# The first sequence's paged values beside the last head's attention, its key pairs afterwards

## The chip, the core and the metric

The kernel runs on one core of a Trainium2 chip. The time is that of one execution on the device in microseconds, from runs of the whole program. One core has five engines that take their instructions in order and wait for each other by semaphores: PE (matrix products), DVE (vector operations), ACT (pointwise functions and copies), POOL (further vector operations) and SP, which here issues nearly all of the transfers between HBM and the on-chip memory.

## The reference

One layer is computed for two batches. The prompt has 1024 rows and 16 meta rows; eight samples have one row each and attend to 4096 past positions, which lie in pages of 128 positions at places that a page table names. Cut to what matters:

```
proj = rms_norm(x) @ w_in                        # q, k, v and the convolution's two inputs
a    = softmax(q1 k1) - lam * softmax(q2 k2)     # 4 heads, two maps each, ALiBi, causal
o    = a @ v                                     # prompt: own keys; sample: 32 pages of keys and values
mix  = concat(rms_norm(o), silu(layer_norm(conv(u)))) @ w_out
x    = x + rms_norm(mix)
y    = x + rms_norm((silu(h @ w_gate) * (h @ w_up)) @ w_down),  h = rms_norm(x)
```

All data are float32. The large products split each operand into a high and a low part and add three products.

## The kernel before

The program is recorded in Python in one long order, and a scheduler then sets the order on each engine by simulated times and priorities; on the chip each engine keeps that order. Three stages matter here.

The **attention** of the prompt runs over 4 heads and 8 blocks of 128 rows (n = 0 to 31; the last head is n = 24 to 31). For a block, PE makes the scores `S` (L507, L508), DVE adds the bias and finds the row's extreme (L509), ACT takes the exponential (L515), DVE joins the two maps (L526), PE transposes the result (`AT`, L534), ACT copies it (L538), and PE multiplies it with the values into `o` (L548). After four blocks, ACT copies `o` to `oh` and squares it (L557, L562), POOL takes the power (`or`, L564), ACT scales (L566), PE transposes (`oT`, L571) and ACT writes `mo` (L573). Beside the last head the eight parts of w_out are loaded (`wo0r` to `wo7r`, on SP, L132) and split by ACT (`wo0H` and on, L138) and POOL (`wo0L` and on, L140).

The **output projection** takes the 8 blocks with 48 products each (tile `mo`, L149 to L151, the same helper as in all large products). Its input rows are loaded as `mx` and split by ACT into `mH` (L900) and by DVE into `mL` (L901). The **FFN** then makes the gate, up and down products (`pg`, `pu`, `dn`), with weights that SP streams in.

The **paged attention** of the eight samples is spread over all of this by a generator, `dec_units`. One unit is a pair of pages, two transfers of 256 KB that SP issues (L665). A key pair is multiplied with the query on POOL (L680, two instructions) and summed on DVE (L690); each sum is recorded only after the next pair's product. A value pair waits until two pairs are there, and then PE makes their four products side by side (`pv`, L732, called a page group here). With one group done, as many key pairs follow as the group had value pairs. Each sequence has 16 key pairs and 16 value pairs. Between a sequence's keys and its values stand a maximum over all partitions on POOL (L707) and the exponential.

How many units are recorded at a place is set by rates: `rate_b` per block of attention (one entry per head), `rate_c` per block of the output projection, `rate_d` per step of the FFN, until all units are used up; then the samples' own rows follow at `rate_s`. At the end of the third head 23 key pairs are recorded, 16 of the first sequence and 7 of the second. A flag, `kv_n[1]`, is false until the last head has been recorded; while it is false, pages go to four buffers, afterwards also to the buffers of the attention's probabilities.

Of the kernel before, what the change touches and what calls it, by code (L numbers as in the profile page):

```python
# [46 lines left out]
def tile_layer(ctx: ExitStack, tc: tile.TileContext, I, O, cfg):  # L47
# [7 lines left out]
    at = ctx.enter_context(tc.tile_pool(name="at", bufs=cfg["at"]))  # L55
# [7 lines left out]
    kv_n = [0, False]  # L63
# [25 lines left out]
    def pdec(name):  # L89
        return ps.tile([P, 512], F32, tag="d", name=name, bufs=cfg["nd"])  # L90
# [564 lines left out]
    def page_pair(src, b, pg, name):  # L655
        t = kv(name)[:, :1024].rearrange("p (i n) -> p i n", i=2)
        for i in range(2):
            n = b * NPG + pg + i
            lds, (v,) = nc.values_load_multi_w_load_instructions(
                pts[0:1, n : n + 1], engines=[SP], min_val=0, max_val=n_pool - 1  # L660
            )
            if len(page_dmas) >= 8:
                for ld in lds:
                    tc.add_manual_dep(ld.ins if hasattr(ld, "ins") else ld, page_dmas[-8], behind, reason="few registers at once")
            x = D.dma_start(t[:, i, :], src[bass.DynSlice(v, 1)].rearrange("o p f -> (o p) f"))  # L665
            if cfg["anchor"] and i == 0:
                tc.add_manual_dep(x.ins if hasattr(x, "ins") else x, point["now"], behind, reason="paced by the prompt's work")
            page_dmas.append(x.ins.name if hasattr(x, "ins") else x.name)
        return t

    def dec_scores(b, st):
        qB = dec.tile([P, 512], F32, tag="qB", name=f"qB{b}")
        D.dma_start(qB, qsD[b].partition_broadcast(P))
        s = dec.tile([P, NPG + 1, 8], F32, tag="s", name=f"s{b}", bufs=3)
        st[b] = s
        for pg in range(0, NPG, 2):
            kt = page_pair(ck, b, pg, f"k{b}_{pg}")
            n = b * NPG // 2 + pg // 2
            for i in range(2):
                x = G.tensor_tensor(kt[:, i, :], kt[:, i, :], qB, op=ALU.mult)  # L680
            products.append((s[:, pg : pg + 2, :], kt))
            if len(products) > cfg["rlag"]:
                head_sums(x)
            yield b
# [3 lines left out]
    def head_sums(after):  # L688
        s, kt = products.pop(0)
        x = V.tensor_reduce(  # L690
            s.rearrange("p a c -> p (a c)"), kt.rearrange("p a (c d) -> p (a c) d", d=HD), axis=AX.X, op=ALU.add
        )
        if after is not None:
            tc.add_manual_dep(x.ins, after.ins.name, behind, reason="sums behind a later product")

    def dec_max(b, st):
        s = st[b]
        V.tensor_tensor(
            s[:, :NPG, :].rearrange("p g (h j) -> p (g h) j", j=2),
            s[:, :NPG, :].rearrange("p g (h j) -> p (g h) j", j=2),  # L700
            dbias.rearrange("p g h -> p (g h)").unsqueeze(2).to_broadcast([P, NPG * NH, 2]), op=ALU.add,
        )
        V.tensor_copy(s[:, NPG, :], selfs[:, b, :])
        m = smt(f"dm{b}", 8, 2)
        V.tensor_reduce(m, s.rearrange("p g c -> p c g"), axis=AX.X, op=ALU.max)
        mg = smt(f"dg{b}", 8, 2)
        G.partition_all_reduce(mg, m, P, bass.bass_isa.ReduceOp.max)  # L707
        st[b] = s, mg

    def dec_exp(b, st):  # L710
        s, mg = st[b]
        V.tensor_tensor(s, s, mg.unsqueeze(1).to_broadcast([P, NPG + 1, 8]), op=ALU.subtract)
        S.activation(s, s, AF.Exp)
        st[b] = s

    def dec_total(b, s):
        V.tensor_reduce(dsum[:, b, :], s.rearrange("p g c -> p c g"), axis=AX.X, op=ALU.add)
        V.tensor_tensor(selfa, selfa, s[:DB, NPG, :], op=ALU.add)

    def dec_values(b, st):  # L720
        a = st.pop(b)
        pv = pdec(f"pv{b}")
        vs = []
        for pg in range(0, NPG, 2):
            if not vs:
                size = min(cfg["vgrp"] if kv_n[1] else 2, (NPG - pg) // 2)
            vs.append((pg, page_pair(cv, b, pg, f"v{b}_{pg}")))
            if len(vs) == size:
                for q, vt in vs:
                    for i in range(2):  # L730
                        g = (q + i) % 4
                        x = T.matmul(  # L732
                            pv[32 * g : 32 * g + 8, :], lhsT=a[:, q + i, :], rhs=vt[:, i, :],
                            start=q + i < 4, stop=q + i >= NPG - 4, tile_position=(0, 32 * g),
                        )
                        if vt is not vs[-1][1]:
                            tc.add_manual_dep(x.ins, page_dmas[-1], together, reason="pages side by side")
                vs = []
            if pg == NPG // 2:
                dec_total(b, a)  # L740
            yield 0 if vs else size
        pvs = dec.tile([P, 512], F32, tag="gs", name=f"pvs{b}", bufs=2)
        for g in range(4):
            S.copy(pvs[32 * g : 32 * g + 8, :], pv[32 * g : 32 * g + 8, :])
            S.dma_start(pvD[b, g], pvs[32 * g : 32 * g + 8, :])

    def dec_units():
        st = {}
        ks = (b for bb in range(DB) for b in dec_scores(bb, st))
        nk, ready, exped, at = 0, 0, 0, []  # L750
        per = NPG // 2

        def softmaxes(all_=False):
            nonlocal ready, exped
            while "k" in nat and ready < (nk - len(products)) // per:
                dec_max(ready, st)
                at.append(nk)
                ready += 1
            while exped < ready and (all_ or nk >= at[exped] + cfg["elag"]):
                dec_exp(exped, st)  # L760
                exped += 1

        def keys(n):
            nonlocal nk
            for _ in range(n):
                if nk < DB * per:
                    next(ks)
                    nk += 1
                    if nk == DB * per:
                        while products:  # L770
                            head_sums(None)
                    softmaxes(nk == DB * per)
                    yield

        yield from keys(per + cfg["lag"])
        while "k" not in nat:
            yield "wait"
        softmaxes(True)
        for b in range(DB):
            for n in dec_values(b, st):  # L780
                yield
                yield from keys(n)

    dgen = dec_units()
    dst = {"done": False}

# [601 lines left out]
    lag=7, rlag=1, elag=2,  # L1388
    xn_g=(), wi_first=1, wi_e=(13, 17), sq=0,
    behind=-400, w0=7, w1=7, wi_n=1, anchor=1, wi_v=(8, 9, 10, 11, 12), taps=11, conv=400, r2_g=1, hb=5,  # L1390
    vgrp=2, fing=5, ml_g=0, fend=22, cst=0, db=3, cn=6, scn=12, wo0=27, wor=2, c0=7,
    at=8, slabs=35, kv=4, p=6, dve_mul=0, rate_b=(1, 1.25, 1, 0.75), rate_c=1, rate_d=2.45, rate_s=2.2,
    ffn_l=lambda nc: nc.vector,
)
_INS = [
# [39 lines left out]
```

## Time and profile before

| | us |
|---|---|
| median of 3 runs (range) | 1439.78 (1434.59 to 1439.84) |
| the profiled execution, whole | 1440.69 |
| its span, from the first to the last instruction | 1438.8 |
| PE busy | 1357.1 (94%) |
| DVE, POOL, ACT busy | 860.9, 595.2, 551.2 |

The span is what the trace covers; some 1.9 us lie around it. PE is busy nearly all the time, so a stretch in which PE waits is where something else sets the time, and a stretch in which it doesn't is as long as PE's work in it. [...]

### The profile page before, as it was taken

What the parts mean: (1) busy time and instruction counts of PE and PEld (TensorE: products, weight loads), DVE (VectorE), ACT (ScalarE), POOL (GpSimd) and SP (SyncE); (2) the same over time, 40 slices, a digit from 0 to 9 for tenths busy, and PEclk for the clock granted to TensorE, in tenths of its full rate; (3) what the DMA queues carried; (4) which work ended last, traced back from release to release, by engine and by line L of the source; (5) the groups of instructions that cost most, each with busy time, mean ns of one, the idle gap of its engine ahead of it and who ended that gap; (6) DMA issues with size and microseconds to landing.
All of it is one profiled execution on the core that took longest, in us unless ns stands there. A gap on an engine that the chain in (4) does not pass through costs nothing.

```text
span 1438.8 us, 21552 instructions
## 1 busy us (share of the span) xinstructions
PE 1357.1 (94%) x6960; PEld 1057.1 (73%) x6960; DVE 860.9 (60%) x1403; ACT 551.2 (38%) x1112; POOL 595.2 (41%) x479
## 2 busy tenths in 40 slices
PE   5999899989869999999999989999999989999997
PEld 5999799979747787777776757676776765666666
DVE  5689996936684567566645465654653374452158
ACT  6566878797764345113021121312121112211122
POOL 4598867445372113745545455464530000000023
PEclk9999999999889999999999999999999999999999
DMA  8211015226535548678867857777677656763454
GB/s 246 86 59 38 27 55 163 75 96 192 170 98 193 171 148 269 211 259 260 262 226 235 265 199 249 235 257 264 204 263 221 214 163 218 229 190 125 147 195 172
DMA packets 199677, 264.34 MB, mean 184 GB/s; under 512 B 16423, under 2 KB 99816, under 8 KB 199557
## 3 DMA queue, kind: packets, MB, share of 16 engines
q1 hardware_dynamic: 188912, 254.40, 54.3%
q10 hardware_dynamic: 10653, 8.57, 1.8%
q8 instruction: 55, 0.90, 0.3%
q14 instruction: 57, 0.47, 0.1%
HBM read 245.92 MB, written 17.48 MB: 183 GB/s over the span
## 4 chain that ended last, share of the span: by engine, by line
PE 59%; SPq 3%; DMA 3%; issue 3%; DVE 3%; POOL 2%; ACT 1%; POOLq 0%; DVEq 0%; ACTq 0%
PE dn L149 5%; PE pu L149 5%; PE dn L150 5%; PE dn L151 5%; PE pu L151 5%; PE pu L150 5%; PE pg L149 5%; PE pg L150 5%; PE pg L151 5%; PE pv L732 4%; PE mo L151 2%; PE mo L149 2%; PE mo L150 2%; DMA v<-in_cache_v 2%; SPq L665 2%
## 5 line engine op out<-in xcount | busy, mean ns | idle before, releaser
L680 POOL TENSOR_TENSOR k<-k,qB 128x512 f32<-128x512 f32 x256 | 353.5, 1409 | 230.2 <-DMA k<-in_cache_k 176.3
L690 DVE TENSOR_REDUCE s<-k 128x16 f32<-128x1024 f32 x128 | 154.8, 1213 | 101.1 <-POOL k L680 100.9
L956 ACT CAST wH<-wr 128x1024 fp32r<-128x1024 f32 x66 | 69.0, 1048 | 239.4 <-DVE wL L958 124.6
L149 PE MATMUL dn<-wH,aH 128*128 128x512 f32 x352 | 141.3, 405 | 5.0 <-DVE y L999 3.4
L149 PE MATMUL pu<-hH,wH 128*128 128x512 f32 x352 | 141.2, 401 | 1.1 <-DVE y L999 1.1
L150 PE MATMUL dn<-wL,aH 128*128 128x512 f32 x352 | 140.9, 400 | 0.0
L151 PE MATMUL pu<-hH,wL 128*128 128x512 f32 x352 | 139.2, 396 | 1.6 <-DVE wL L958 1.6
L151 PE MATMUL dn<-wH,aL 128*128 128x512 f32 x352 | 140.7, 400 | 0.0
L149 PE MATMUL pg<-hH,wH 128*128 128x512 f32 x352 | 140.4, 399 | 0.0
L150 PE MATMUL pu<-hL,wH 128*128 128x512 f32 x352 | 140.1, 398 | 0.0
L150 PE MATMUL pg<-hL,wH 128*128 128x512 f32 x352 | 139.3, 396 | 0.0
L151 PE MATMUL pg<-hH,wL 128*128 128x512 f32 x352 | 139.2, 395 | 0.0
L958 DVE TENSOR_TENSOR wL<-wr,wH 128x1024 fp32r<-128x1024 f32 x66 | 93.7, 1420 | 46.3 <-ACT wH L956 22.2
L999 DVE TENSOR_TENSOR y<-dn,y 128x512 f32<-128x512 f32 x144 | 95.5, 684 | 38.0 <-PE dn L151 37.1
L414 POOL TENSOR_TENSOR cb<-cb 128x512 f32<-128x512 f32 x80 | 102.9, 1316 | 18.0 <-ACT cb L413 9.9
L1071 POOL TENSOR_TENSOR y<-y,wfpost 128x512 f32<-128x512 f32 x10 | 17.6, 1772 | 206.7 <-ACT ft L1069 206.6
L423 DVE SCALAR_TENSOR_TENSOR acc<-u,cw,acc 128x512 f32<-128x512 f32 x144 | 98.7, 747 | 0.2
L982 ACT CAST aH<-sg 128x512 fp32r<-128x512 f32 x44 | 27.3, 620 | 167.6 <-DVE sg L975 167.5
L149 PEld LDWEIGHTS dn<-wH,aH 128*128 128x128 f32 x352 | 67.5, 192 | 31.8 <-DVE y L999 6.8
L149 PEld LDWEIGHTS pu<-hH,wH 128*128 128x128 f32 x352 | 66.4, 189 | 29.4 <-issue 12.9
L975 DVE TENSOR_TENSOR sg<-sg,pu 128x512 f32<-128x512 f32 x44 | 30.1, 683 | 94.0 <-PE pu L151 94.0
L149 PEld LDWEIGHTS pg<-hH,wH 128*128 128x128 f32 x352 | 66.1, 188 | 27.4 <-issue 11.6
(581 smaller groups left out, 2969.5 us busy)
## 6 DMA issues: line engine op xcount, KB each, us to landing
k<-in_cache_k SPq DMA_DIRECT2D x256, 256.0 KB
v<-in_cache_v SPq DMA_DIRECT2D x256, 256.0 KB
wr<-in_w_gate SPq DMA_DIRECT2D x22, 512.0 KB
wr<-in_w_up SPq DMA_DIRECT2D x22, 512.0 KB
wr<-in_w_down SPq DMA_DIRECT2D x22, 512.0 KB
sd<-in_w_down SPq DMA_DIRECT2D x22, 512.0 KB
sw_gate<-in_w_gate SPq DMA_DIRECT2D x20, 512.0 KB
sw_up<-in_w_up SPq DMA_DIRECT2D x20, 512.0 KB
```

The source lines that it names most:

```text
L149: T.matmul(out, lhsT=wH, rhs=xH, start=first, stop=False)
L150: T.matmul(out, lhsT=wH, rhs=xL, start=False, stop=False)
L151: mark(T.matmul(out, lhsT=wL, rhs=xH, start=False, stop=last))
L414: G.tensor_tensor(accp, accp, t, op=ALU.add)
L423: V.scalar_tensor_tensor(dst, src, cw[:, ct, k : k + 1], acc, op0=ALU.mult, op1=ALU.add)
L680: x = G.tensor_tensor(kt[:, i, :], kt[:, i, :], qB, op=ALU.mult)
L690: x = V.tensor_reduce(s.rearrange("p a c -> p (a c)"), kt.rearrange("p a (c d) -> p (a c) d", d=HD), axis=AX.X, op=ALU.add)
L732: x = T.matmul(pv[32 * g : 32 * g + 8, :], lhsT=a[:, q + i, :], rhs=vt[:, i, :], start=q + i < 4, stop=q + i >= NPG - 4, tile_position=(0, ...
L956: S.copy(H[:, :1024], raw[:, :1024])
L958: V.tensor_tensor(L[:, :1024], raw[:, :1024], H[:, :1024].bitcast(F32), op=ALU.subtract)
L975: V.tensor_tensor(sg, sg, o, op=ALU.mult)
L999: V.tensor_tensor(y[b][:, ws], o, y[b][:, ws], op=ALU.add)
```

## The change

Two edits. In `dec_units`, the key pairs that are due before a sequence's values are recorded ahead of them in one piece (this sum is zero for the first sequence and, as the counts come out, for the third and later ones), and no key pairs follow a page group while the flag is false. The rate of the last head goes from 0.75 to 2 units per block, 16 units instead of 6.

```
--- before.py
+++ after.py
@@ -777,9 +777,11 @@
             yield "wait"
         softmaxes(True)
         for b in range(DB):
+            yield from keys(per * (b + 1) + cfg["lag"] - nk)
             for n in dec_values(b, st):
                 yield
-                yield from keys(n)
+                if kv_n[1]:
+                    yield from keys(n)
 
     dgen = dec_units()
     dst = {"done": False}
@@ -1389,7 +1391,7 @@
     xn_g=(), wi_first=1, wi_e=(13, 17), sq=0,
     behind=-400, w0=7, w1=7, wi_n=1, anchor=1, wi_v=(8, 9, 10, 11, 12), taps=11, conv=400, r2_g=1, hb=5,
     vgrp=2, fing=5, ml_g=0, fend=22, cst=0, db=3, cn=6, scn=12, wo0=27, wor=2, c0=7,
-    at=8, slabs=35, kv=4, p=6, dve_mul=0, rate_b=(1, 1.25, 1, 0.75), rate_c=1, rate_d=2.45, rate_s=2.2,
+    at=8, slabs=35, kv=4, p=6, dve_mul=0, rate_b=(1, 1.25, 1, 2), rate_c=1, rate_d=2.45, rate_s=2.2,
     ffn_l=lambda nc: nc.vector,
 )
 _INS = [
```

So all 16 value pairs of the first sequence are recorded beside the last head, and the second sequence gets 16 key pairs in a row, 8 of them in the output projection. What the scheduler makes of it is seen at three places.

On PE, at the end of the last head's attention, before the change (`S` are scores, `AT` and `oT` transposes, `o` the attention's output, `pv` the page products, `mo` the output projection; the digits name head and block):

```order
L548 MATMUL o34_5156<-vm_113,metaT0_115 128x128
L534 MATMUL AT370_5398<-ident_75,p370_5364 128x128 x4
L548 MATMUL o34_5156<-V3_4125,ats360_5300 128x128 x3
L534 MATMUL AT374_5406<-ident_75,p370_5364 128x128 x4
L548 MATMUL o34_5156<-V3_4125,ats364_5308 128x128 x4
L534 MATMUL AT378_5413<-ident_75,p370_5364 128x128
L548 MATMUL o34_5156<-vm_113,metaT1_116 128x128
L548 MATMUL o34_5156<-V3_4125,ats370_5403 128x128 x3
L548 MATMUL o34_5156<-V3_4125,ats374_5411 128x128 x4
L149 MATMUL mo00_5455<-wo4H_5232,mH0_5445 128x512
```

and after it:

```order
L548 MATMUL o34_5280<-V3_4125,ats364_5508 128x128 x4
L534 MATMUL AT378_5640<-ident_75,p370_5591 128x128
L548 MATMUL o34_5280<-vm_113,metaT1_116 128x128
L548 MATMUL o34_5280<-V3_4125,ats370_5630 128x128 x3
L548 MATMUL o34_5280<-V3_4125,ats374_5638 128x128 x4
L548 MATMUL o34_5280<-V3_4125,ats378_5642 128x128
L732 MATMUL pv0_4904<-v0_20_5418,s0_2014 8x512 x2
L732 MATMUL pv0_4904<-v0_22_5441,s0_2014 8x512 x2
L732 MATMUL pv0_4904<-v0_24_5540,s0_2014 8x512 x2
L732 MATMUL pv0_4904<-v0_26_5563,s0_2014 8x512 x2
L571 MATMUL oT37_5835<-ident_75,oh37_5653 128x128 x4
L149 MATMUL mo00_5682<-wo4H_5408,mH0_5672 128x512
```

Seven page groups now stand ahead of the first `mo`, where there was one; the last two of them follow the last `o`, and so does `oT37`, which stood among the first products of `mo`.

On ACT at the same place, before:

```order
L538 COPY ats360_5300<-AT360_5295 128x384
L538 COPY ats364_5308<-AT364_5303 128x512
L900 CAST mH0_5445<-mo33_5221 128x128
L538 COPY metaT1_116<-AT370_5398 16x128
L538 COPY ats370_5403<-AT370_5398 128x384
L900 CAST mH0_5445<-mx00_5334 128x384
L538 COPY ats374_5411<-AT374_5406 128x512
L900 CAST mH0_5445<-mx01_5335 128x512
L538 COPY ats378_5415<-AT378_5413 128x128
L557 COPY oh37_5426<-o34_5156 128x4x128
```

and after (`mx` is `mo00`'s input, `mH0` its high part; lines are two further down):

```order
L538 COPY ats374_5638<-AT374_5633 128x512
L538 COPY ats378_5642<-AT378_5640 128x128
L557 COPY oh37_5653<-o34_5280 128x4x128
L138 CAST wo6H_5520<-wo6r_5518 128x1024
L562 ACTIVATE junk_1744,ssq3_4874<-oh37_5653 128x129 x4
L566 ACTIVATE oh37_5653<-oh37_5653,or37_5660 128x128 x4
L138 CAST wo7H_5526<-wo7r_5524 128x1024
L573 ACTIVATE mo37_5840<-oT37_5835,sublnT_85 128x512
L902 CAST mH0_5672<-mx01_5535 128x512
L902 CAST mH0_5672<-mx00_5534 128x384
L902 CAST mH0_5672<-mo33_5397 128x128
```

The splits of `wo6` and `wo7` and the whole end of the last four blocks (`oh37` to `mo37`) now come before the first `mH0`.

On SP, the last transfers that the start of the output projection needs, after the change:

```order
L887 DMA mx10_5666<-mixT_90 128x3x128 [waits DMAHW1_49,PE_49]
L887 DMA mx11_5667<-mixT_90 128x4x128 [waits DMAHW2_49,Activation_49]
L665 ISA
L665 DMA v0_26_5563<-in_cache_v 128x512 [waits DMAHW3_49,PE_49]
L665 ISA
L665 DMA v0_26_5563<-in_cache_v 128x512 [waits DMAHW4_49]
L132 DMA wo7r_5524<-in_w_out 128x1024 [waits DMAHW5_49]
```

The load of `wo7`, which stood ahead of the second sequence's ninth key pair, now stands behind the pair `v0_26`, whose buffer comes free with a page group.

## Rows read from the trace of the kernel before

**Rows 1.** The page: span of the profiled execution

```profile
span 1438.8 us, 21552 instructions
```

**Rows 2.** Busy time by stretch: us, busy us (instructions) per engine, PE clock, DMA share, GB/s

```profile
382.00:442.20 60.20, 39.72 (x232) 35.19 (x232) 41.70 (x100) 35.95 (x96) 30.56 (x18) 0.76 0.44 145
442.20:538.90 96.70, 96.70 (x453) 77.28 (x452) 53.03 (x93) 36.22 (x96) 19.88 (x23) 1.00 0.51 165
602.60:671.60 69.00, 69.00 (x320) 49.64 (x319) 39.90 (x44) 13.50 (x16) 32.20 (x25) 1.00 0.78 252
```

**Rows 3.** Timeline of PE in the output projection: start us, us, engine, line, operation

```profile
456.39 0.39 PE L149 MATMUL mo<-wo7H,mH 128*128 128x512 f32 x1
456.62 0.40 PE L150 MATMUL mo<-wo7L,mH 128*128 128x512 f32 x1
456.95 1.04 PE L732 MATMUL pv<-v,s 128*8 128x512 f32 x8
457.92 0.50 PE L151 MATMUL mo<-wo7H,mL 128*128 128x512 f32 x1
```

**Rows 4.** Timeline of PE at the end of the last head's attention

```profile
433.87 0.48 PE L571 MATMUL oT<-ident,oh 128*128 128x128 f32 x1 [4.84 <-ACT oh L566]
...
440.71 1.73 PE L548 MATMUL o<-V,ats 128*128 128x128 f32 x14
442.19 0.47 PE L149 MATMUL mo<-wo4H,mH 128*128 128x512 f32 x1
```

**Rows 5.** Timeline of POOL in the same stretch

```profile
425.61 2.35 POOL L140 TENSOR_TENSOR wo6L<-wo6r,wo6H 128x1024 fp32r<-128x1024 f32 x1 [1.00 <-ACT wo6H L138]
427.92 1.60 POOL L680 TENSOR_TENSOR k<-k,qB 128x512 f32<-128x512 f32 x1
429.48 2.92 POOL L140 TENSOR_TENSOR wo7L<-wo7r,wo7H 128x1024 fp32r<-128x1024 f32 x1
432.37 1.01 POOL L564 TENSOR_TENSOR or<-ssq,mhalf 128x4 f32<-128x4 f32 x1
```

**Rows 6.** Timeline of ACT in the same stretch

```profile
424.50 1.03 ACT L138 CAST wo6H<-wo6r 128x1024 fp32r<-128x1024 f32 x1
...
425.70 0.59 ACT L557 COPY oh<-o 128x512 f32<-128x512 f32 x1
...
427.17 0.31 ACT L562 ACTIVATE junk<-oh 128x129 f32<-128x129 f32 x1
...
427.60 0.31 ACT L562 ACTIVATE junk<-oh 128x129 f32<-128x129 f32 x1
...
433.41 1.28 ACT L566 ACTIVATE oh<-oh,or 128x128 f32<-128x128 f32 x4 [3.74 <-POOL or L564]
...
436.73 0.69 ACT L573 ACTIVATE mo<-oT,sublnT 128x512 f32<-128x512 f32 x1 [1.24 <-PE oT L571]
...
440.22 0.62 ACT L900 CAST mH<-mx 128x512 fp32r<-128x512 f32 x1
```

**Rows 7.** Timeline of the SP queue: issue of page and weight transfers

```profile
424.35 0.89 SPq L665 DMA_DIRECT2D k<-in_cache_k  x2
```

**Rows 8.** What the SP queue waited for, 380 to 445 us: us in total, times, longest

```profile
SPq L665 <- PE pv L732: 17.0, 1, 17.0
```

**Rows 9.** Timeline of the SP queue before a late page group in the FFN

```profile
839.79 1.90 SPq L665 DMA_DIRECT2D v<-in_cache_v  x4
```

**Rows 10.** Timeline of PE at that page group

```profile
845.18 1.89 PE L732 MATMUL pv<-v,s 128*8 128x512 f32 x8 [6.79 <-DMA v<-in_cache_v]
...
848.43 0.40 PE L150 MATMUL dn<-wL,aH 128*128 128x512 f32 x1
```

**Rows 11.** Timeline of PE: first and last page group of the second sequence

```profile
602.64 1.05 PE L732 MATMUL pv<-v,s 128*8 128x512 f32 x8
...
671.62 1.04 PE L732 MATMUL pv<-v,s 128*8 128x512 f32 x8
```

**Rows 12.** What PE waited for, 668 to 1200 us

```profile
PE pv L732 <- DMA v<-in_cache_v: 10.9, 6, 6.8
```

More of the change, by code (lines that the diff above doesn't have):

```diff
@@ L779, in dec_units @@
         for b in range(DB):
+            yield from keys(per * (b + 1) + cfg["lag"] - nk)
             for n in dec_values(b, st):
                 yield
-                yield from keys(n)
+                if kv_n[1]:
+                    yield from keys(n)
     dgen = dec_units()
@@ L1391 @@
     vgrp=2, fing=5, ml_g=0, fend=22, cst=0, db=3, cn=6, scn=12, wo0=27, wor=2, c0=7,
-    at=8, slabs=35, kv=4, p=6, dve_mul=0, rate_b=(1, 1.25, 1, 0.75), rate_c=1, rate_d=2.45, rate_s=2.2,
+    at=8, slabs=35, kv=4, p=6, dve_mul=0, rate_b=(1, 1.25, 1, 2), rate_c=1, rate_d=2.45, rate_s=2.2,
     ffn_l=lambda nc: nc.vector,
```

## The prediction

> **What bounds the kernel now.** I read the busy times by stretch first, then what PE waited for, then the timelines of all engines between 380 and 445 us. PE sets the time in the output projection and the FFN: from 442.2 to 538.9 us it is busy for 96.7 of 96.7 us at the full clock, and the same holds for 602.6 to 671.6 us [rows 2]. From 382 to 442.2 us, the last head, it is busy for 39.7 of 60.2 us and its clock is 0.76, while DVE has 41.7 us of work; transfers move 145 GB/s there, against 252 in the FFN [rows 2]. So there is room on PE and on the transfers in the last head, and none on PE afterwards. The change moves work across that border, at 442.19 us, where the first product of `mo` starts [rows 4].
>
> **What a page group costs.** In the output projection one group runs for 1.04 us [rows 3]. Between the starts of the products around it lie 457.92 - 456.62 = 1.30 us, against 456.62 - 456.39 = 0.23 us between neighbours [rows 3]. A group costs PE 1.30 - 0.23 = 1.07 us.
>
> **Step 1, groups that leave the bound stretch.** Before, one group of the 64 stands ahead of `mo`; after, seven do. Six groups x 1.07 = 6.4 us less after the border. Their cost is certain as long as PE is the limit there. The key pairs that come instead into the output projection cost PE nothing: POOL is busy for 19.9 and DVE for 53.0 of 96.7 us [rows 2], and some four more pairs, at two products of up to 1.60 us each [rows 5], fit on POOL.
>
> **Step 2, small work that now lies ahead.** Four transposes `oT37` and two products `o` stood among `mo` and now precede it: 0.8 us less (14 instructions of `o` take 1.73 us [rows 4], so four of them some 0.3, and the transposes about as much again).
>
> **Step 3, the last head up to its last `o`.** Before, PE stood for 4.84 us until 433.87 us for the scaled `oh` [rows 4], ACT waited 3.74 us of that for the power on POOL [rows 6], and POOL had the split of `wo7` (2.92) and a key product (1.60) ahead of it [rows 5]. After, neither of the two is ahead of it any more, nor are the key products of the last head's second half there at all. I expect PE to pass that transpose about 4 us sooner. Against it stand the page groups in front: buffers. One of the four is held by the seventh key pair, whose sum waits for the next product, so a group and a half fit; the queue of SP already waited 17.0 us for a page group [rows 8], and the next pages were issued only at 424.35 us [rows 7]. Now each pair is issued when an earlier group ends. From the first of four transfers to the group that waits for them lie 845.18 - 839.79 = 5.4 us, from the last, 845.18 - 841.69 = 3.5 us [rows 9, 10]. A page is thus usable about 0.9 + 3.5 = 4.4 us after the group that freed its buffer (0.89 us for the two issues [rows 7]). The groups stand 4 to 8 us apart until the third, and nearer after it, so I give back about 1 us of the 4 and take 3 us sooner, last `o` near 439. Bounds: 6 us sooner (pages never late, DVE also free of the key products on POOL) and 3 us later (three groups each 2 us late, no gain).
>
> **Step 4, the seam.** This is what speaks against the change. Before, the splits of `mo`'s first input ran on ACT between the copies (0.62 us at 440.22 [rows 6]), and `mo` followed the last `o` directly. After, ACT does these one after another behind the last `o`: copy 0.59, split of `wo6` 1.03, four squares at 0.43 each (1.7; they lie beside the split of `wo6` on POOL, 2.35, which stands ahead of the power), power 1.01, scaling 1.28, split of `wo7` 1.03, `mo37` 0.69, first `mH` 0.62 [rows 5, 6]. On the longest path: 0.59 + 1.03 + 2.35 + 1.01 + 1.28 + 1.03 + 0.69 + 0.62 = 8.6 us. `wo7` is in time for its place: it is issued behind `v0_26`, about 2.2 us after the last `o`, and lands by the estimate above at about 6, when ACT has reached it. PE has two groups (2.1 us) in these 8.6 us, already counted as outside the bound stretch, and idles for the rest. Bounds: 5 us, if the splits are ready while ACT still waits for something else, and 13 us, if the input `mx1`, ahead of `v0_26` on SP, waits for a buffer for another 4 us, about PE's own longest wait in this place (4.84 [rows 4]).
>
> The clock adds to it: after a wait of 6.79 us in the FFN, products ran at half speed from 845.18 to 848.43 us, where the mean falls back to 0.40 [rows 10]; half of these 3.2 us is lost, 1.6 us. After the wait of 4.84 us before 433.87, on the other hand, the first `mo` starts at 0.47, close to full speed, 8 us later [rows 4], so nothing need be lost if work fills the time. I take 1 us, with 0 and 2 as ends. [...]
>
> **Step 5, the FFN.** Ten units, or four steps' worth of them, are gone before it starts, so the paged attention ends about 20 us earlier. That by itself is worth nothing: the samples' rows that follow are done before the end already. PE waited 10.9 us for pages in six places [rows 12]. These depend on how the pages meet the weights and on the stop of POOL at each sequence's maximum, which all come again at other places. I take 0, with -7 and +9 as ends.
>
> **Sum.** -6.4 - 0.8 - 3 + 8.6 + 1 + 0 = -0.6 us. On the profiled execution (span 1438.8 [rows 1], 1440.69 in all) this gives 1440.1; the median of the runs lies 0.9 below that execution, so I forecast **1439 us**. A measurement of this kernel can tell about 0.5%, 7.2 us, from no change; the forecast is no change, and its own range is 1433 to 1446.
>
> **Rivals.**
>
> *The seam stays small and waits in the FFN fall away.* If the pages are never late, the last `o` comes 6 us sooner, the seam takes 5, and of the 10.9 us [rows 12] some 3 are gone: -6.4 - 0.8 - 6 + 5 + 0 - 3 = -11, some 1429 us. For it: DVE and POOL lose work in the stretch where PE waits. Against it: the order on ACT shows the chain behind the last `o` plainly.
>
> *The second sequence's pages can't keep up (slower).* Its eight groups took from 602.64 to 671.62 us [rows 11], 69.0 us, at 252 GB/s [rows 2], so 17.4 MB. In the new order on PE 221 products instead of 263 stand between the first and the last of them: 42 x 0.23 = 9.7 us less, 59.3 us, for which 293 GB/s would be needed. If 252 is all that the queue gives there, PE waits 9.7 us, and loses about 1.6 to the clock: -0.6 + 11.3 = +10.7, some 1450 us. It decides as soon as the pages held in buffers when that sequence begins cover less than some 3 us of it. For it: 293 GB/s is above every stretch of [rows 2]. Against it: POOL and DVE are only half busy there, the keys of that stretch come earlier, in the output projection, where only 165 GB/s flow [rows 2], and ten buffers can run ahead.
>
> *The change does not do what it says* (key pairs left among the groups, or the groups pushed out of the last head): the order on PE excludes it, and I give it no chance.
>
> **How the numbers follow.** Forecast 0.60, first rival 0.19, second 0.13, and 0.08 for a seam at its upper end with pages late as well (+3 + 4.4 + 3 = +10, about 1449). With that faster 0.19, same 0.60, slower 0.21. For 8 in 10 the range takes in most of both rivals: 1430 to 1450.
>
> **What would show it.** Right: seven page groups ahead of the first `mo` and 57 after it; the transpose `oT33` about 4 us sooner than 433.87; the last `o` near 439 and the first `mo` near 447 to 448, with PE idle between for some 6 us and ACT busy with the chain of step 4; then a stretch up to the end that is 6 to 7 us shorter. Wrong: a first `mo` at or before 443, which would make the change a gain of its whole step 1, or later than 455; a wait for pages of several us in the second sequence's groups; or a changed sum of PE's waits in the FFN, which would make step 5 the largest term.

## The result and the profile after

The changed kernel is slower: 1462.63 us median (1460.51 to 1463.47, 4 runs) against 1437.18 us (1434.24 to 1439.84, 4 runs); ratio 1.017, 95% interval 1.0143 to 1.0196. The profiled span is 1461.6 us, 22.8 more than [rows 1]. The forecast was 1439.

Busy time by stretch of the kernel after (us, then busy us and instructions of PE, PEld, DVE, ACT, POOL, then PE's granted clock as a share of full speed, DMA share, GB/s):

```profile
449.80:546.50 96.70, 96.68 (x434) 78.02 (x435) 59.87 (x98) 34.83 (x88) 29.06 (x31) 0.98 0.56 183
546.50:600.00 53.50, 40.09 (x177) 31.70 (x175) 37.67 (x49) 18.10 (x33) 31.50 (x22) 0.87 0.59 203
600.00:680.00 80.00, 69.13 (x303) 48.54 (x302) 44.15 (x49) 12.88 (x16) 39.45 (x30) 0.89 0.67 217
```

The last two of these stretches in the kernel before:

```profile
546.50:600.00 53.50, 53.50 (x255) 40.04 (x254) 34.21 (x46) 19.73 (x33) 28.41 (x24) 1.00 0.78 255
600.00:680.00 80.00, 80.00 (x371) 57.66 (x370) 48.30 (x52) 18.14 (x24) 41.00 (x30) 1.00 0.77 249
```

The output projection is as full as in [rows 2], only 7.6 us later. Behind it, where PE never stood before, it now stands for 13.4 us up to 600 and for 10.9 us up to 680. What it waits for between 450 and 700 us (us in total, times, longest):

```profile
PE hT L875 <- DVE z L921: 12.9, 1, 12.9
PE pu L151 <- DVE wL L960: 7.4, 1, 7.4
PE pu L149 <- ACT wH L958: 3.2, 1, 3.2
```

The seam, on PE (start, us, operation, idle before and its cause), to be read against [rows 4]:

```profile
430.15 0.33 PE L571 MATMUL oT<-ident,oh 128*128 128x128 f32 x1 [0.97 <-ACT oh L566]
...
436.55 1.95 PE L548 MATMUL o<-V,ats 128*128 128x128 f32 x16
440.48 1.65 PE L732 MATMUL pv<-v,s 128*8 128x512 f32 x8 [1.99 <-DMA mx<-mixT]
445.59 1.90 PE L732 MATMUL pv<-v,s 128*8 128x512 f32 x8 [3.46 <-DMA v<-in_cache_v]
447.42 1.12 PE L571 MATMUL oT<-ident,oh 128*128 128x128 f32 x4
449.82 0.80 PE L149 MATMUL mo<-wo4H,mH 128*128 128x512 f32 x1 [1.28 <-ACT mH L902]
```

`oT33` comes 3.7 us sooner, and the last `o` ends near 438.5. Then two page groups wait, the second for its pages (the profile puts the first wait down to `mx`, which a group doesn't read). The first `mo` is at 449.8, 2 us later than forecast. ACT waits in the same place, for the load of `wo7` that stands behind the last pages on SP; the scaling of `oh37` ended near 444.9:

```profile
447.33 1.05 ACT L138 CAST wo7H<-wo7r 128x1024 fp32r<-128x1024 f32 x1 [2.48 <-DMA wo7r<-in_w_out]
```

The large wait is made on POOL and DVE. DVE of the kernel after, around the second sequence's maximum (L707 on POOL, subtracted by L712 on DVE):

```profile
559.14 0.14 DVE L123 TENSOR_SCALAR hr_t<-hs 128x1 f32<-128x1 f32 x1
...
571.31 0.43 DVE L712 TENSOR_TENSOR s<-s,dg 128x264 f32<-128x264 f32 x1 [5.59 <-POOL dg L707]
581.39 2.29 DVE L921 SCALAR_TENSOR_TENSOR z<-xr,hr_r,wffn 128x1024 f32<-128x1024 f32 x1 [9.65 <-POOL hr_r L125]
583.61 1.07 DVE L880 TENSOR_TENSOR hL<-hT,hH 128x256 fp32r<-128x256 f32 x3
```

and POOL of the same stretch:

```profile
560.09 3.61 POOL L680 TENSOR_TENSOR k<-k,qB 128x512 f32<-128x512 f32 x2 [4.33 <-DMA k<-in_cache_k]
570.88 0.40 POOL L707 PARTITION_ALL_REDUCE dg<-dm  x1 [7.17 <-issue]
580.77 0.59 POOL L125 TENSOR_TENSOR hr_r<-hr_t,mhalf 128x1 f32<-128x1 f32 x1 [9.50 <-issue]
581.35 21.92 POOL L680 TENSOR_TENSOR k<-k,qB 128x512 f32<-128x512 f32 x14
```

The all-reduce works for 0.40 us and takes POOL away for 7.17 us ahead of it and 9.50 behind it. Behind it in POOL's order stands `hr7`, the norm of the last block of the output projection; its input was ready at 559.3, its result comes at 581.4, and PE stands at that block's transpose (behind that wait, from 583.74 to 587.49 us, its granted clock was 0.50). This time of POOL without other work around an all-reduce is called a stop below. The same maximum in the kernel before, on DVE:

```profile
564.24 0.75 DVE L878 TENSOR_TENSOR hL<-hT,hH 128x256 fp32r<-128x256 f32 x2
569.95 0.43 DVE L712 TENSOR_TENSOR s<-s,dg 128x264 f32<-128x264 f32 x1 [4.96 <-POOL dg L707]
...
580.21 1.22 DVE L690 TENSOR_REDUCE s<-k 128x16 f32<-128x1024 f32 x1 [4.98 <-POOL k L680]
```

and on POOL:

```profile
556.39 5.59 POOL L680 TENSOR_TENSOR k<-k,qB 128x512 f32<-128x512 f32 x4 [7.51 <-DMA k<-in_cache_k]
569.52 0.39 POOL L707 PARTITION_ALL_REDUCE dg<-dm  x1 [7.54 <-DMA k<-in_cache_k]
577.62 10.52 POOL L680 TENSOR_TENSOR k<-k,qB 128x512 f32<-128x512 f32 x8 [7.70 <-PE pv L732]
```

It comes at nearly the same time, and DVE is held twice there too, for 4.96 and 4.98 us. But `hr7` was made at 547.1 and the splits `hL` of the last block are done at 565.0, so PE loses nothing. Ahead of the sixteen all-reduces of the two kernels POOL shows no work for 5.7 to 8.7 us, waits for data included, and behind them for 6.8 to 9.5 us at the fourteen that are followed by other work. What POOL does in these times no run shows; besides the all-reduces, the kernel after has only two records of that line (L707) for each, of at most 20 ns:

```profile
L707 POOLq MODIFY_POOL_CONFIG  x16: 1/8/20, 383.0 to 1066.1; - x16
```

The third sequence's maximum holds DVE twice as well, and here the splits `wL` of the next weights stand behind it, PE's second wait (DVE of the kernel after):

```profile
650.90 0.43 DVE L712 TENSOR_TENSOR s<-s,dg 128x264 f32<-128x264 f32 x1 [5.51 <-POOL dg L707]
...
660.89 1.22 DVE L690 TENSOR_REDUCE s<-k 128x16 f32<-128x1024 f32 x1 [6.03 <-POOL k L680]
662.02 6.79 DVE L960 TENSOR_TENSOR wL<-wr,wH 128x1024 fp32r<-128x1024 f32 x3
```

PE's third wait, 3.2 us for `wH`, hangs on the same stop: ACT's split comes behind the exponential, which waited for the subtraction until 651.4. Before, this maximum came at 653 us, and PE was busy all the time around it.

### The profile page after: what moved, and what is told of

It reads as the page before. It is cut to its first block, busy times and chain, and to the rows that moved or that the text cites. A ratio compares the mean times of both kernels' runs of the same rounds, so it can differ in the third digit from the quotient of the medians.

```text
span 1461.6 us, 21580 instructions
## 1 busy us (share of the span) xinstructions
PE 1362.1 (93%) x6960; PEld 1057.9 (72%) x6960; DVE 859.3 (59%) x1403; ACT 551.1 (38%) x1112; POOL 596.8 (41%) x479
## 5 line engine op out<-in xcount | busy, mean ns | idle before, releaser
L680 POOL TENSOR_TENSOR k<-k,qB 128x512 f32<-128x512 f32 x256 | 359.1, 1429 | 235.2 <-DMA k<-in_cache_k 180.6
L149 PE MATMUL dn<-wH,aH 128*128 128x512 f32 x352 | 138.3, 397 | 1.6 <-ACT wH L958 1.6
L151 PEld LDWEIGHTS pu<-hH,wL 128*128 128x128 f32 x352 | 66.6, 189 | 31.6 <-DVE wL L960 9.1
L151 PEld LDWEIGHTS dn<-wH,aL 128*128 128x128 f32 x352 | 66.0, 188 | 26.9 <-issue 11.2
L732 PE MATMUL pv<-v,s 128*8 128x512 f32 x512 | 71.2, 630 | 13.2 <-DMA v<-in_cache_v 11.1
```

Source lines behind the costliest of these rows:

```text
L149: T.matmul(out, lhsT=wH, rhs=xH, start=first, stop=False)
L151: mark(T.matmul(out, lhsT=wL, rhs=xH, start=False, stop=last))
L732: x = T.matmul(pv[32 * g : 32 * g + 8, :], lhsT=a[:, q + i, :], rhs=vt[:, i, :], start=q + i < 4, stop=q + i >= NPG - 4, tile_position=(0, ...
```

## The experiments

A kernel's name stands with its first `mo` and the time from there to the end, both from its profiled run. Kernels with the same order up to `mo` differ there by up to 6 us (e2 and e13): 3.0 us of it are there already ahead of the last head, some 2 come from the pages. So the column of the first `mo` is good to some 6 us only.

| kernel | median us | ratio to before | first mo | mo to end |
|---|---|---|---|---|
| before | 1436 to 1440 | 1 | 442.2 | 996.6 |
| after | 1462.6 | 1.017 | 449.8 | 1011.8 |
| e1 maximum behind the norm | 1466.6 | 1.019 | 449.6 | 1014.5 |
| e2 after, no all-reduce | 1421.2 | 0.988 | 436.9 | 981.9 |
| e3 key piece alone | 1447.2 | 1.006 | 440.3 | 1003.9 |
| e4 rate alone | 1463.9 | 1.017 | 455.6 | 1008.1 |
| e5 before, no all-reduce | 1411.9 | 0.981 | 430.6 | 980.2 |
| e6 second all-reduce left out | 1452.3 | 1.010 | 448.5 | 1002.0 |
| e7 maximum late | 1456.1 | 1.012 | 451.6 | 1003.4 |
| e8 after, maximum on PE | 1433.9 | 0.996 | 440.2 | 992.2 |
| e9 e2, keys early | 1429.7 | 0.994 | 440.8 | 986.6 |
| e10 e2, w_out early | 1423.3 | 0.989 | 441.0 | 980.0 |
| e11 before, maximum on PE | 1419.0 | 0.987 | 434.4 | 982.5 |
| e12 mended, first try | 1443.2 | 1.003 | 437.2 | 998.2 |
| e13 e2, keys thinned | 1417.8 | 0.984 | 442.9 | 975.7 |
| e14 e2, six buffers | 1434.9 | 0.997 | 449.2 | 983.2 |
| e15 mended, second try | 1440.3 | 1.001 | 454.5 | 984.1 |
| e16 after, keys thinned | 1448.1 | 1.006 | 448.7 | 989.5 |
| e17 thinned, maximum on PE | 1421.1 | 0.990 | 436.7 | 981.2 |

**e1: the order of one norm.**
```diff
-        G.partition_all_reduce(mg, m, P, bass.bass_isa.ReduceOp.max)
+        x = G.partition_all_reduce(mg, m, P, bass.bass_isa.ReduceOp.max)
+        if b == 1:
+            tc.add_manual_dep(x.ins, norm["hr7"], behind, reason="maximum behind the last norm")
```

The lines that note the norm's instruction in `norm` are left out here.

> The changed kernel with one order more: POOL's all-reduce for the second sequence's maximum stands behind the power of the last block's norm (hr7), as it did before the change; on DVE, z of block 7 then stands ahead of the subtraction of that maximum. Nothing else is moved. Theory 1 (that all-reduce ahead of hr7 stops PE at hT for 12.9 us and costs the clock after it): the wait of hT for z falls below 3 us, the median falls from 1462.6 by 13 to 17 us, to 1446 to 1450. Rival A (the slow start of the output projection, 7.6 us later than before, is the loss, and the later waits only take up slack): 1459 to 1463. Rival B (the rate of pages and weights in the FFN sets the end; PE would wait for pages or weights instead): hT's wait falls, but the median falls by 0 to 5 us only.

Measured: no gain, 1466.6. The wait of `hT` fell to 1.4 us, and PE stood one step later (waits, 450 to 700 us):

```profile
PE pg L152 <- DVE hL L884: 18.5, 1, 18.5
PE pu L153 <- DVE wL L964: 6.1, 1, 6.1
```

DVE of e1 shows why:

```profile
571.08 0.43 DVE L716 TENSOR_TENSOR s<-s,dg 128x264 f32<-128x264 f32 x1 [4.54 <-POOL dg L709]
571.43 1.08 DVE L884 TENSOR_TENSOR hL<-hT,hH 128x256 fp32r<-128x256 f32 x3
583.86 1.22 DVE L692 TENSOR_REDUCE s<-k 128x16 f32<-128x1024 f32 x1 [11.35 <-POOL k L682]
```

DVE took its work in the given order, and the sum of the next key product (L692) waited 11.35 us for POOL. The remaining `hL` stand behind that sum. Theory 1 fell in its form: not that one norm, but all that DVE makes at the turn from projection to FFN is behind the stop (theory 2). The second row of PE's waits is the third sequence's maximum, as in the kernel after.

**e2 and e5: no all-reduce, in the kernel after and before.** Both leave the maximum out and subtract a zero.
```diff
-        G.partition_all_reduce(mg, m, P, bass.bass_isa.ReduceOp.max)
+        G.memset(mg, 0.0)
```


> The changed kernel without the maximum over the partitions: a zero is subtracted from the scores instead of it (DVE's subtraction and maxima stay), so all eight all-reduces on POOL are gone. Theory 1 (the stop of POOL around an all-reduce is what PE waits for, at 570 us and, for the third sequence, at 640 to 680): both stalls go, 12.9 us at hT and 7.4 + 3.2 at pu; with the clock 23 to 28 us less, 1434 to 1440. Rival A (slow start of the output projection): within 4 us of 1462.6. Rival B (weights come late behind pages at 640 to 680): the stall at hT goes, that at pu stays, 1446 to 1451.

> The kernel before without the maximum over the partitions (a zero is subtracted, as in e2). Theory 2 (each all-reduce takes POOL away for some 17 us and holds DVE at two places for some 16 us; it costs time only where PE in that window needs what DVE has not made yet, and the change moved the second and third onto such places): the kernel before loses little to its stops, so 1425 to 1435, and the change is then worth 4 to 14 us less once the stops are gone (e2: 1421.2). Rival C (the stops cost both kernels much the same, and the change itself is a loss): 1400 to 1412, so that the change stays 10 to 20 us slower without stops too.

Measured: 41.4 us less in the kernel after, 28.6 less in the kernel before (1440.5 in that comparison). By the table the first all-reduce, in the last head, costs both about the same: the first `mo` is 12.9 and 11.6 us sooner, of which 3.3 and 1.3 are there already before that all-reduce. Behind `mo` the stops cost 1011.8 - 981.9 = 29.9 us after the change and 996.6 - 980.2 = 16.4 before it: 13.5 of the 22.8 us. Both theory 2 (the stops fell on worse places) and rival C (the change is a loss in itself) hold a part: without stops the change still costs 9.3 us, 6.3 up to `mo` and 1.7 behind it by the spans (the 6.3 with the uncertainty of that column). In e5 PE waits for no pages behind `mo`; the 10.9 us of [rows 12] went with the stops. The edit also lets the scheduler move other instructions: of the 1403 on DVE, 85 stand elsewhere in e2 and 44 in e5. So these prices hold the stops together with that.

**e3 and e4: each half alone.** e3 is the kernel after with `rate_b[3]` at 0.75, e4 the kernel before with it at 2.

> One half of the change: key pairs in one piece behind the first sequence's values, but with the old rate in the last head (0.75), so two page groups before the last o instead of five and none between it and the first mo; the all-reduce of the second sequence stands behind hr7 again. Theory 1: no stall at hT; no seam; 1433 to 1440, as the kernel before. Rival A (slow start of the output projection): as before too, 1437. Rival B (from the second sequence on, pages come closer together because keys of the second sequence come first in one piece): 1444 to 1452.

> The other half: two steps a tile in the last head, but key pairs still between the groups of values; four page groups ahead of the first mo (three before the last o, one behind it), and the all-reduce of the second sequence far ahead, still before hr6 (whose transpose comes later than that of block 5). Theory 1: the stop of POOL falls on blocks 5 and 6 of the output projection, whose transposes stand further ahead of their use, so it costs 0 to 5 us; the seam costs half of that of the changed kernel, the moved groups give back 3: 1434 to 1444. Rival A (seam): 1440 to 1446. Rival B: as the kernel before, 1437.

Measured: e3 lost 7.3 us behind `mo`, more than theory 1 gave it; its time lies in the range of rival B, and PE's waits for pages come to 13.0 us, those for `wL` to 6.3. e4 was outside all three forecasts, as slow as the whole change: its maximum lies in the middle of the projection (513 us), and PE waited 6.8 us for `mH` there. Each half moves the stops, so each has places of its own; the halves don't add up.

**e6 and e7: only the second maximum left out, or made later.** In e6 a zero is subtracted for the second sequence alone; e7 has `rate_c=0.5`.

> The changed kernel without the all-reduce of the second sequence alone (zero subtracted for it); the other seven stay. Theory 2: the stall at the turn from output projection to FFN (12.9 us and the clock after it) falls to 0 to 5 us, as in e2; the third sequence's stall at 640 to 680 may stay or fall elsewhere: 1440 to 1450. Rival A (slow start of the output projection makes the loss): 1459 to 1463. Rival D (the loss is spread over all eight stops, so that one of them is an eighth of 41 us): 1456 to 1459.

> The changed kernel with half as many key pairs per block of the output projection (0.5 instead of 1), so that the second sequence's maximum comes later: on POOL behind hr7, and on DVE its subtraction stands behind all splits of block 7's transposes (in the changed kernel it stands ahead of z of block 7, in e1 directly behind it). All eight all-reduces stay. Theory 2: the stall at hT and hL goes, 1438 to 1450, with the stop now beside the first units' second halves, which may cost up to 8 us there. Rival A (seam): 1456 to 1463. Rival B (pages now come later, so PE waits for pages of the second sequence): 1460 to 1470.

Measured: 10.3 and 6.5 us less than the kernel after, short of what theory 2 expected; e7 lies at the edge of rival A's range. In e6 the wait for `hL` is still 4.7 us, with no stop near it, and the third maximum costs 8.9 us at a product that waits for DVE's `y`. In e7 the turn is clean, and PE waits 16.0 us for pages in four places between 452 and 800 us, against 10.9 in six places of [rows 12] over a longer stretch. In both, another wait grew when one stop was taken out or moved.

**e8 and e11: the maximum on PE.** Everything is computed. e11, in the kernel before (e8 has a diagonal and ones instead of the broadcast):
```diff
-        G.partition_all_reduce(mg, m, P, bass.bass_isa.ReduceOp.max)
+        pt = pb(f"dmT{b}")
+        T.transpose(out=pt[:8, :P], in_=m, identity=ident)
+        mx = smt(f"dx{b}", 1)
+        V.tensor_reduce(mx[:8], pt[:8, :P], axis=AX.X, op=ALU.max)
+        mg = pb(f"dg{b}")[:, :8]
+        T.matmul(mg, lhsT=mx[:8].to_broadcast([8, P]), rhs=ident[:8, :8], start=True, stop=True)
```


> The changed kernel with the maximum over the partitions made without POOL: PE transposes the 128 maxima of eight columns, DVE reduces and puts them on a diagonal, and a product with ones spreads them; everything is computed. The order puts five page groups ahead of the first mo (four before the last o). Theory 2: POOL is not stopped, so 1420 to 1430: e2's time plus 16 small products and 16 small operations of DVE, some 0.3 us each where they show. Rival C: 1425 to 1440, and not faster than the kernel before by more than 0.5%. Rival B: 1440 or more, the FFN being held by pages.

> The kernel before with the maximum over the partitions made without POOL: PE transposes the maxima, DVE reduces them, and one product with the identity spreads them. Theory 2/3 (stops of POOL cost the kernel before some 28 us, e5): 1412 plus 16 small products and what PE waits for them, some 0 to 1.5 us for each of 8: 1414 to 1426. If PE waits longer for DVE's part of each maximum, up to 1436.

Measured: e11 1419.0, ratio 0.987 (0.9845 to 0.9895), faster than both kernels, as expected. e8 is 1433.9, above the range of theory 2 and inside that of rival C: PE still waits 6.1 us at the turn, for `hH`.

**e9, e10, e13: what is left without stops.** All on e2: `rate_c=2.3` (e9), `wo0=26` (e10), and in e13
```diff
-            fill()
+            fill() if n >= 3 else dec_step(1)
```


> e2 (the changed kernel, a zero subtracted instead of the maximum) with 2.3 key pairs per block of the output projection instead of 1, so that the 16 pairs of the piece are through before the projection ends. Theory 3 (without the stops, the changed kernel loses some 10 us at the turn from projection to FFN, because the rest of the piece, 12 to 14 key products in a row, falls on the stretch where DVE makes the splits for the FFN's first units): the waits at 560 to 580 go, 1409 to 1414. Rival E (that stall is pages arriving late, or simply work that has to be paid somewhere): 1418 to 1424.

> e2 with the loads and splits of w_out begun one tile earlier, so that on ACT the split of wo6 is no longer behind the last o, and the scaled oT37 stands behind the input of the first block. Theory 3 (the seam is the chain of ACT behind the last o): first mo 2 to 4 us sooner than in e2 (436.9), 1416 to 1419. Rival F (the seam is held by the last two page groups, whose pages come late behind mx): first mo within 1 us of 436.9, 1420 to 1422.

> e2 (the changed kernel, a zero subtracted instead of the maximum) with one step instead of 2.45 behind each of the FFN's first three units, so that the rest of the key piece no longer falls on the turn in one run. Theory 4 (the turn's stall is the density of key pairs there: POOL 20 of 20 us busy, DVE 20 of 20): the wait for hL (5.2 us) and its cold clock go, 1409 to 1414. Rival E (pages or the late start of the projection set the turn): within 3 us of e2's 1421.2.

POOL of e2 at the turn, the case that these three act on:

```profile
554.40 19.39 POOL L680 TENSOR_TENSOR k<-k,qB 128x512 f32<-128x512 f32 x12
```

Twelve key products in a row, and DVE without a pause from 540 to 570. Up to 600, PE is busy for 54.4 of 60 us. e9 put the pairs earlier and lost: between 450 and 560 us PE waited 7.4 us for `mH` and 5.1 for `mL`, inside the projection. Theory 3 had the mechanism, but the wrong cure, since a dense run of pairs hurts there as well. e13 thinned them: the wait for `hL` at the turn falls from 5.2 to 1.5 us, the granted clock from 560 to 580 us rises from 0.83 to 1.00, and the time from `mo` to the end by 6.2 us, as theory 4 had it. Its median falls by only 3.5, to 1417.8, short of theory 4's range: in the profiled run its first `mo` came 6.0 us later. Of these, 3.0 are there ahead of the last head, and some 2 come from the wait for pages ahead of the last group (6.11 us, 4.16 in e2). Busy time of 540 to 600 us in e2 and in e13:

```profile
sum 60.00, PE 54.44 PEld 41.73 DVE 40.21 ACT 19.44 POOL 38.58; mean PE 18.15 PEld 13.91 DVE 13.40 ACT 6.48 POOL 12.86
```

```profile
sum 60.00, PE 57.47 PEld 45.60 DVE 46.00 ACT 22.12 POOL 38.92; mean PE 19.16 PEld 15.20 DVE 15.33 ACT 7.38 POOL 12.97
```

e10 didn't shorten the seam, and both forecasts for its first `mo` missed (441.0). The split of `wo6` is out of the chain behind the last `o`, but that of `wo7` now stands ahead of the scaling of `oh`; it waits 2.44 us for the load of `wo7`, and PE waits 4.6 us for the scaled `oh`.

**e12, e14 to e17: mending the change.** e14 is e2 with `kv=6, slabs=33`; e12 is the kernel after with e11's maximum, e9's and e10's edit; e15 with e11's, e13's and e14's; e16 with e13's alone; e17 with e11's and e13's.

> The changed kernel with all three causes mended: the maximum on PE and DVE as in e11, 2.3 key pairs per block as in e9, w_out one tile earlier as in e10. Theory 3: the seam, the turn and the stops are gone, what is left is the six groups ahead of mo: 1408 to 1420, no slower than e11 by more than 3 us. Rival: if the change costs time in itself beyond these, 5 us or more above e11.

> e2 with six page buffers instead of four in the last head, and two slabs fewer. Theory 4 (the six groups are not hidden in the last head because each page pair is issued only when a buffer comes free, 7.3 us of waits for pages up to the first mo): those waits fall below 3 us, first mo 4 to 7 us sooner than in e2 (436.9), so 430 to 433, and the time 1414 to 1418, the turn's stall staying. Rival G (the pages are late by the queue, not by the buffers, or the two slabs are missed later): first mo within 2 us of 436.9, 1419 to 1430.

> The changed kernel, everything computed: the maximum on PE and DVE as in e11, one step behind each of the FFN's first three units as in e13, six page buffers as in e14. Theory 4: the six groups are hidden, the turn is free, no stops: 1409 to 1416, 3 to 10 us below e11 (1419.0). Rival: 1417 to 1425, the change worth nothing when mended.

> The changed kernel with its all-reduces and only the one edit of e13 (one step behind each of the FFN's first three units). The second sequence's maximum comes at or after the turn then. Theory 4: the turn's density falls, but the stop of some 17 us lies there still; 1445 to 1456. If the stop comes behind the turn altogether: 1436 to 1444. Rival A (late start of the projection is the loss): 1458 to 1463.

> The changed kernel, everything computed: the maximum on PE and DVE as in e11, and one step behind each of the FFN's first three units as in e13; four page buffers, w_out where the change has it. Theory 4 (what is left of the change is a later start of the projection, 6 to 10 us, against 6 to 7 us less behind it): 1418 to 1426, within 7 us of e11 (1419.0) and not below it by more than 2. If the six groups are a gain after all: 1408 to 1415. If the change costs more than stops and density: 1428 or more.

e16 is the changed kernel with one line altered, and takes back 14.5 of the 25.5 us, in the range of theory 4. Its runs spread widely (1439.3 to 1457.4); the profiled one is among the fastest. e12 and e15 were no faster than the kernel before, each by a second edit: e12 carries e9's wait for `mH` (9.1 us inside the projection), e15 starts `mo` at 454.5, as e14 does at 449.2. With six buffers the waits for pages up to `mo` fall from 7.3 to 3.1 us, but e14 is 14.5 us behind e2 already ahead of the last head (last `nk` transposes of the samples' keys at 386.1 and 371.6); of its two edits, the two slabs fewer are the likelier reason, which isn't shown. From there to `mo` it takes 2.1 us less than e2, so e14 leaves open whether the six groups could be hidden there. e17 has neither edit, and ends where theory 4 put it: 1421.1, ratio 0.990 (0.9872 to 0.9921), beside e11's 0.987. Mended in this way, the change is worth nothing. The thinning of e13 was not tried in the kernel before.

## Why the prediction was wrong

The step that failed is step 5, "I take 0, with -7 and +9 as ends": it names the stops of POOL and puts their change at nothing. Behind the first `mo` the forecast had 6.4 + 0.8 = 7.2 us less, and 15.2 more came: a miss of 22.4 us, nearly the whole. By e2 and e5, 13.5 us of it are the stops; 8.9 stay without them, 6.2 of these by e13 from step 1.

- *Step 1* counted the groups rightly, and what it set against them wrongly: "the key pairs ... cost PE nothing", because POOL and DVE were half idle over the projection. The pairs come in one piece, and its end falls on the turn, where POOL then makes 12 products in a row and DVE has no pause (e2). e13 prices that at 6.2 us. With it mended, `mo` to the end is 975.7 against 980.2 in e5, 4.5 of the 7.2 us; how much thinning would give the kernel before isn't known.
- *Step 2* was small and isn't told apart by any run. Its working is off: at 1.73 us for 14, four products take 0.5 us and two take 0.25, not 0.3 for four.
- *Step 3* was right: `oT33` 3.7 us sooner (forecast 4), the last `o` near 439.
- *Step 4* had the right mechanism and was 2 us short: the first `mo` at 449.8 instead of 447 to 448. The chain of ACT was there, but the pages came last: PE waited 1.99 and 3.46 us at the last two groups, and "`wo7` is in time for its place" failed with them, since its load stands behind `v0_26`: ACT waited 2.48 us for it, until 447.3. The clock cost more than the 1 us taken: the granted clock was 0.50 from 449.8 to 454.25 and 0.98 from there to 460; ten products of `mo` started in these 4.4 us, which at the 0.23 us between later ones take 2.3, so some 2.1 us are lost. The prediction's "so nothing need be lost if work fills the time" came from a misread row: after the wait of 4.84 us before 433.87 the granted clock was 0.50 up to 438.6 and 0.97 from there to 442.2, so the products behind that wait were slowed as well, only ahead of `mo`, much as those behind the 6.79 us in the FFN (0.51 from 845.18 to 848.43).
- *Step 5* saw that the stops of POOL come at other places, and then let gains and losses cancel. They didn't: at the stops looked at, 15 to 17 us on POOL, DVE loses 10 to 16, and PE lost nothing only where what it needed next from DVE was made already. Before, all but the first of the eight cost 16.4 us; after, 29.9. The last of the prediction's signs of being wrong, a changed sum of PE's waits in the FFN, is what came. Where each falls could have been read from the order: in the changed kernel `hr7` stands behind the second all-reduce, in the kernel before ahead of it.
- *The rival of pages* (1450) was the right side for the wrong reason: in the kernel after, the waits for pages behind `mo` came to 6.4 us, less than before. They grew to 16.0 us in e7.

Not settled: how the 13.5 us divide over the seven later stops. e6 gives 10.3 for leaving out the second one, but the third then cost more as well. The 1.3 us of the 22.8 that are left, 7.6 up to `mo` against 6.3 without stops, are within the uncertainty of that column.

## What to carry to other kernels

An operation that takes an engine away for long cost nothing or a lot here (for the second maximum, no wait of PE or one of 12.9 us), by what stood behind it on each engine that waited for it; a change of order has to be read at each such place, not only where it is made. A mean busy share over a stretch doesn't show that work fits: look at the ten or twenty us in which it will land. And a stop that can be taken out altogether (e11: 1.3%) is worth more than any place found for it.

## What the runs showed of the hardware

An all-reduce over the partitions of 128x8 works for 0.39 to 0.40 us on POOL, and POOL does no other work for 15.6 to 17.1 us around it at the second maximum (561.98 to 577.62 us in the kernel before, 563.7 to 580.77 after), 13.4 to 17.1 at the fourteen of both kernels that are followed by other work. Leaving all eight out made the kernel before 28.6 us faster (e5). The same maximum by two small products on PE and one reduction on DVE brings in 21 of these (e11).
